# A two-layer decoder step: the weight sums of a Strassen product, three by accumulating DMAs and one on GpSimd

## The chip, the core and the metric

The kernel runs on one core of a Trainium2 chip. The metric is the device time of one execution in microseconds, median of three runs. A core has TensorE (PE, with its weight loads shown as PEld), VectorE (DVE), ScalarE (ACT), GpSimd (POOL) and SyncE (SP). SP issues nearly all loads. GpSimd computes elementwise and also issues the accumulating DMAs, which read a tile in on-chip memory and add it to another. Each engine works through its own instructions in order.

## What is computed

One step of a decoder with two layers for 576 tokens (512 of a prompt, 64 sampled). Of each layer only two products matter here: the gates of the merge, and the first product of the feed-forward block.

```
proj = (h @ lw['w_in']).astype(f32)          # 1024 of its columns for each of four gate blocks
gates = jax.nn.sigmoid(gate_logits.reshape(B, L, N_BRANCH, D_MODEL))
merged = jnp.sum(gates * up, axis=2).astype(h.dtype)
y = merged @ lw['w_out']
...
h = _rmsnorm(x, lw['ffn_norm'])
g, u = jnp.split(h @ lw['w_ffn_in'], 2, axis=-1)
x = x + ((jax.nn.silu(g) * u) @ lw['w_ffn_out']).astype(x.dtype)
```

The model width is 1024, so a product sums over 8 blocks of 128 rows; the feed-forward width is 2816, that is 22 blocks of 128 columns for `g` and 22 for `u`.

## The kernel before

Every float32 operand is split into two float16 parts, high and low. ScalarE writes the high part (L1692), VectorE the low part (L1693, it reads both the float32 source and the high part), and TensorE makes three matmuls for each block (L1718 to L1720: high by high, high by low, low by high).

**Strassen pairs.** Two column blocks of 128 are taken as one pair, cut in two along the rows: `a11`, `a12` are the two halves of the rows of the first column block, `a21`, `a22` those of the second. Each is a tile of 128 x 512 float32 (256 KB). The tokens are cut into two halves of 288. Instead of eight products of halves the pair takes seven: three with the weights themselves (A11, A12, A22) and four with sums of weights (S1 to S4). Each product is 12 matmuls of 128 x 128 by 288 columns, so a pair has 84. There are 27 pairs in a layer: 8 in the stage of the last two gate blocks (`last_gates`) and 19 in the feed-forward stage (`ffn`, column blocks 3 to 21).

**The preparation of a pair** is the generator `strassen_weights` (L1684). It loads the four tiles, then makes the sums in place, each in a step of its own:

- step 2, L1698: `a21 += a22`, by an accumulating DMA that GpSimd issues (S1)
- step 3: A11 is split, then GpSimd computes `a11 = a21 - a11` (S2)
- step 4: A22 is split, then GpSimd computes `a22 = a22 - a11` (S3)
- step 5: A12 is split, then GpSimd computes `a12 = a12 - a11` (S4)
- steps 6 to 9: S2, S1, S3 and S4 are split (`hS` tiles)

The three sums on GpSimd go through the helper at L1696. A sum overwrites the tile that a split has just read, so it waits for VectorE's low part.

**The products of a pair** are made by `strassen` (L1708) in the order A11, A12, A22, S2, S1, S3, S4. After each product one step of the preparations is taken: the first four steps split S2, S1, S3, S4 of the pair at hand, the last four run steps 2 to 5 of the next pair. VectorE combines the products (`plus`, L1734): `u2 = p1 + S2`, `u4 = u2 + S1`, and so on. In the gate stage ScalarE then takes the tanh of each result (L1529), and VectorE multiplies it with the branch's product (`gu`, L1539). In the feed-forward stage follow the silu (`fsg`, L1763) and the product (`fy`, L1765).

**Order and buffers.** A scheduler places the instructions of each engine; the order is fixed before the run. The loads of a pair are issued two pairs ahead, on SP. The tiles come from rings: "raw" has 4 buffers, "w" 4, "rd" 2 of 512 KB. In the feed-forward stage even column blocks take three raw and one w tile (L1787), odd ones two rd tiles (L1779). A load into a buffer waits until the buffer's last reader or writer is done. Matmuls write to PSUM rings; ring "b" has 4 buffers and "g" and "r" 2 each, and a buffer comes free when VectorE or ScalarE has read it.

Of the kernel before, what the change touches and what calls it, by code (L numbers as in the profile page):

```python
# [16 lines left out]
ADD, SUB, MUL, MAX, MIN = ALU.add, ALU.subtract, ALU.mult, ALU.max, ALU.min  # L17
# [157 lines left out]
class Net:  # L175
# [14 lines left out]
    def t(self, ring, shape, name, dt=F32):  # L190

        assert int(np.prod(shape[1:])) * (2 if dt == F16 else 4) <= SIZE[ring], (shape, name)
        return self.rings[ring].tile(list(shape), dt, tag=ring, name=name)
# [51 lines left out]
    def split(self, out_hi, out_lo, src, scale=1.0):  # L245

        nc = self.nc
        nc.scalar.activation(out_hi, src, AF.Copy, scale=scale)
        if scale == 1.0:
            nc.vector.tensor_tensor(out_lo, src, out_hi, op=SUB)  # L250
        else:
            nc.vector.scalar_tensor_tensor(out_lo, src, scale, out_hi, op0=MUL, op1=SUB)
# [1431 lines left out]
    def strassen_weights(self, key, load, ring, **rings):  # L1684

        nc = self.nc
        a11, a12, a21, a22 = load()
        w = self.sw[key] = {}

        def split(name, a):  # L1690
            hl = w[name] = self.t(rings.get(name, ring), [128, 2, 4, 128], "h" + name, F16)
            nc.scalar.activation(hl[:, 0], a, AF.Copy, scale=WS)  # L1692
            nc.vector.scalar_tensor_tensor(hl[:, 1], a, WS, hl[:, 0], op0=MUL, op1=SUB)  # L1693

        def add(dst, a, b, op):
            nc.gpsimd.tensor_tensor(dst, a, b, op=op)  # L1696
        yield
        nc.gpsimd.dma_start(out=a21, in_=a22, accum_op=ADD)  # L1698
        yield
        for name, a, op0, op1 in (("A11", a11, a21, a11), ("A22", a22, a22, a11), ("A12", a12, a12, a11)):  # L1700
            split(name, a)
            add(a, op0, op1, SUB)
            yield
        for name, a in (("S2", a11), ("S1", a21), ("S3", a22), ("S4", a12)):
            split(name, a)
            yield

    def strassen(self, w, t, prep, ps3, ring, then=None):  # L1708


        nc = self.nc
        h0, h1 = slice(0, HW), slice(HW, T)

        def product(ring, a, rhs):
            ps = self.psum(ring, [128, HW], "fs" + a)
            for k in range(4):
                hi, lo = rhs(k)
                nc.tensor.matmul(ps, w[a][:, 0, k], hi, start=k == 0, stop=False)  # L1718
                nc.tensor.matmul(ps, w[a][:, 0, k], lo, start=False, stop=False)  # L1719
                nc.tensor.matmul(ps, w[a][:, 1, k], hi, start=False, stop=k == 3)  # L1720
                if k % 2:
                    yield
            next(prep, None)
            return ps

        def b(o, hs):
            return lambda k: (self.h[k + o][:, 0, hs], self.h[k + o][:, 1, hs])

        def tt(i):
            return lambda k: t(i, k)  # L1730

        def plus(a, p, name):
            o = self.t(ring if name[1] == "c" else "gt", [128, HW], name)
            nc.vector.tensor_tensor(o, a, p, op=ADD)  # L1734
            if then and name[1] == "c":
                then(o)
            return o
        p1 = self.t("gt", [128, HW], "sp1")
        nc.scalar.copy(p1, (yield from product("b", "A11", b(0, h0))))
        c11 = plus(p1, (yield from product("b", "A12", b(4, h0))), "sc11")  # L1740
        p4 = yield from product("g", "A22", tt(3))
        u2 = plus(p1, (yield from product("b", "S2", tt(1))), "su2")
        p5 = yield from product("g", "S1", tt(0))
        u4 = plus(u2, p5, "su4")
        u3 = plus(u2, (yield from product(ps3, "S3", tt(2))), "su3")
        c22 = plus(u3, p5, "sc22")
        c21 = plus(u3, p4, "sc21")
        c12 = plus(u4, (yield from product(ps3, "S4", b(4, h1))), "sc12")
        return c11, c12, c21, c22
# [193 lines left out]
```

## Time and profile before

| what | value |
|---|---|
| time before, median of 3 runs | 2242.47 us (2237.26 to 2242.92) |
| profiled execution, its own time | 2235.82 us |
| its span, first to last instruction | 2234.1 us |
| busy share of the span | TensorE 92%, VectorE 75%, ScalarE 48%, GpSimd 29% |
| mean granted TensorE clock | 0.975 of full speed |
| gate stage of the pairs, layer 0 and 1 | about 536 to 677 us and 1629 to 1773 us |
| feed-forward stage of the pairs, layer 0 and 1 | about 782 to 988 us and 1878 to 2086 us |

The profile is of one execution; the rows read from it stand in a section below. Busy time of TensorE is modelled: a matmul is shown as 0.29 us long, while in a full stretch a new one starts every 0.12 us. Idle time is shown in brackets behind a row, with the engine whose work ended it.

### The profile page before, as it was taken

What the parts mean: (1) busy time and instruction counts of PE and PEld (TensorE: products, weight loads), DVE (VectorE), ACT (ScalarE), POOL (GpSimd) and SP (SyncE); (2) the same over time, 40 slices, a digit from 0 to 9 for tenths busy, and PEclk for the clock granted to TensorE, in tenths of its full rate; (3) what the DMA queues carried; (4) which work ended last, traced back from release to release, by engine and by line L of the source; (5) the groups of instructions that cost most, each with busy time, mean ns of one, the idle gap of its engine ahead of it and who ended that gap; (6) DMA issues with size and microseconds to landing.
All of it is one profiled execution on the core that took longest, in us unless ns stands there. A gap on an engine that the chain in (4) does not pass through costs nothing.

```text
span 2234.1 us, 42266 instructions
## 1 busy us (share of the span) xinstructions
PE 2047.3 (92%) x15754; PEld 1616.7 (72%) x15754; DVE 1677.4 (75%) x3719; ACT 1070.6 (48%) x2400; POOL 652.0 (29%) x850
## 2 busy tenths in 40 slices
PE   7988899898989999999998889889998988999998
PEld 5766676686767677777776667768776766777776
DVE  7889856868786899973488996686687768998531
ACT  6554545436454655442466344363554455554332
POOL 2212212245550544320011131222365415443000
PEclk9999999999999999999999999999999999999999
DMA  6312213333436244343421222142344443443431
GB/s 179 82 36 66 54 52 91 94 77 84 108 100 200 59 118 126 88 132 108 120 69 51 54 56 60 51 116 72 79 98 104 124 144 93 118 116 93 126 105 50
DMA packets 373497, 209.58 MB, mean 94 GB/s; under 512 B 59810, under 2 KB 360410, under 8 KB 373292
## 3 DMA queue, kind: packets, MB, share of 16 engines
q1 hardware_dynamic: 365516, 192.73, 31.1%
q0 software_dynamic: 7776, 14.16, 3.5%
q8 instruction: 124, 2.03, 0.4%
q14 instruction: 81, 0.66, 0.1%
HBM read 173.72 MB, written 16.59 MB: 85 GB/s over the span
## 4 chain that ended last, share of the span: by engine, by line
PE 47%; DVE 31%; ACT 8%; issue 7%; DMA 4%; POOL 3%; SPq 0%; DVEq 0%; ACTq 0%; POOLq 0%
PE pb L243 4%; PE pb L241 4%; PE pb L242 4%; PE xb L243 4%; PE xb L242 4%; PE xb L241 4%; DVE hA L1693 3%; DVE hS L1693 2%; DVE whl L229 2%; DVE sc L1734 2%; DVE fy L1765 2%; DVE qg L1111 2%; PE fsS L1720 2%; PE fsS L1718 2%; PE fsS L1719 2%
## 5 line engine op out<-in xcount | busy, mean ns | idle before, releaser
L241 PE MATMUL pb<-h,whl 128*128 128x288 f16 (+1 forms) x1504 | 439.9, 293 | 3.7 <-ACT h L463 2.2
L243 PE MATMUL pb<-h,whl 128*128 128x288 f16 (+1 forms) x1504 | 439.7, 293 | 2.7 <-DVE whl L229 2.7
L242 PE MATMUL pb<-h,whl 128*128 128x288 f16 (+1 forms) x1504 | 439.5, 292 | 0.6 <-DVE h L464 0.4
L229 DVE SCALAR_TENSOR_TENSOR whl<-raw,whl 128x512 f16<-128x512 f32 (+1 forms) x352 | 251.7, 725 | 132.0 <-ACT whl L228 130.3
L243 PEld LDWEIGHTS <-whl 128*128 128x128 f16 (+1 forms) x2784 | 277.3, 100 | 88.4 <-issue 11.0
L242 PEld LDWEIGHTS <-whl 128*128 128x128 f16 (+1 forms) x2784 | 276.7, 99 | 87.4 <-issue 11.0
L241 PEld LDWEIGHTS <-whl 128*128 128x128 f16 (+1 forms) x2784 | 279.0, 100 | 77.0 <-issue 3.6
L228 ACT ACTIVATE whl<-raw 128x512 f16<-128x512 f32 (+1 forms) x352 | 213.0, 616 | 167.4 <-PE pb L243 58.1
L243 PE MATMUL xb<-fa,whl 128*128 128x288 f16 x704 | 201.3, 286 | 0.0
L242 PE MATMUL xb<-fa,whl 128*128 128x288 f16 x704 | 201.3, 286 | 0.0
L241 PE MATMUL xb<-fa,whl 128*128 128x288 f16 x704 | 201.3, 286 | 0.0
L1718 PE MATMUL fsA<-h,hA 128*128 128x288 f16 x432 | 123.5, 286 | 14.4 <-DVE gu L1539 9.1
L1718 PE MATMUL fsS<-st,hS 128*128 128x288 f16 x456 | 131.1, 287 | 6.0 <-ACT hS L1692 6.0
L1720 PE MATMUL fsS<-st,hS 128*128 128x288 f16 x456 | 131.2, 288 | 0.9 <-DVE hS L1693 0.9
L1719 PE MATMUL fsS<-st,hS 128*128 128x288 f16 x456 | 131.1, 287 | 0.0
L1720 PE MATMUL fsA<-h,hA 128*128 128x288 f16 x432 | 123.6, 286 | 1.6 <-DVE hA L1693 1.6
L1719 PE MATMUL fsA<-h,hA 128*128 128x288 f16 x432 | 123.5, 286 | 0.0
L1696 POOL TENSOR_TENSOR raw<-raw 128x512 f32<-128x512 f32 x52 | 79.5, 1529 | 133.8 <-DVE hA L1693 129.7
L1718 PEld LDWEIGHTS <-hS 128*128 128x128 f16 x864 | 85.1, 99 | 35.5 <-ACT hS L1692 14.1
L1693 DVE SCALAR_TENSOR_TENSOR hA<-sraw,hA 128x512 f16<-128x512 f32 x110 | 101.5, 930 | 10.4 <-ACT hA L1692 9.7
L1696 POOL TENSOR_TENSOR sraw<-sraw 128x512 f32<-128x512 f32 x60 | 89.9, 1501 | 50.0 <-DVE hA L1693 45.5
L1720 PEld LDWEIGHTS <-hS 128*128 128x128 f16 x864 | 85.2, 99 | 24.6 <-DVE hS L1693 3.0
(487 smaller groups left out, 5271.1 us busy)
## 6 DMA issues: line engine op xcount, KB each, us to landing
raw<-in_w_in SPq DMA_DIRECT2D x208, 256.0 KB
sraw<-in_w_ffn_in SPq DMA_DIRECT2D x40, 512.0 KB
raw<-in_w_ffn_out SPq DMA_DIRECT2D x80, 256.0 KB
raw<-in_w_ffn_in SPq DMA_DIRECT2D x78, 256.0 KB
x<-xd SPq DMA_DIRECT2D x32, 288.0 KB
raw<-sraw POOLq DMA_DIRECT2D x34, 256.0 KB, 3.3
sraw<-in_w_in SPq DMA_DIRECT2D x32, 256.0 KB
raw<-in_w_out SPq DMA_DIRECT2D x32, 256.0 KB
```

Source lines behind the costliest of these rows:

```text
L228: nc.scalar.activation(hl[:, 0, :n], raw[:, :n], AF.Copy, scale=WS)
L229: nc.vector.scalar_tensor_tensor(hl[:, 1, :n], raw[:, :n], WS, hl[:, 0, :n], op0=MUL, op1=SUB)
L241: nc.tensor.matmul(ps, wh, hi, start=i == 0, stop=False)
L242: nc.tensor.matmul(ps, wh, lo, start=False, stop=False)
L243: nc.tensor.matmul(ps, wl, hi, start=False, stop=i == len(ks) - 1)
L1111: nc.vector.tensor_tensor(qo, qq, ee, op=MUL)
L1693: nc.vector.scalar_tensor_tensor(hl[:, 1], a, WS, hl[:, 0], op0=MUL, op1=SUB)
L1696: nc.gpsimd.tensor_tensor(dst, a, b, op=op)
L1718: nc.tensor.matmul(ps, w[a][:, 0, k], hi, start=k == 0, stop=False)
L1719: nc.tensor.matmul(ps, w[a][:, 0, k], lo, start=False, stop=False)
L1720: nc.tensor.matmul(ps, w[a][:, 1, k], hi, start=False, stop=k == 3)
L1734: nc.vector.tensor_tensor(o, a, p, op=ADD)
```

## The change

Before, one sum of a pair was an accumulating DMA and three were subtractions on GpSimd. After, S1 stays as it was; S2 stays on GpSimd, with its sign turned round (`a11 = a11 - a21`); S3 and S4 become accumulating DMAs of the turned `a11` (`a22 += a11`, `a12 += a11`). The sign of S2 is taken back where its product is used: `u2 = p1 - S2`. The values are the same sums. So in each of 54 pairs two GpSimd subtractions of 128 x 512 become two DMAs of 256 KB that GpSimd issues. All accumulating DMAs now stand at one line (L1696 of the changed kernel), the one subtraction at L1701, and lines further down are numbered 5 higher.

```diff
@@ strassen_weights
-        def add(dst, a, b, op):
-            nc.gpsimd.tensor_tensor(dst, a, b, op=op)
-        yield
-        nc.gpsimd.dma_start(out=a21, in_=a22, accum_op=ADD)
-        yield
-        for name, a, op0, op1 in (("A11", a11, a21, a11), ("A22", a22, a22, a11), ("A12", a12, a12, a11)):
-            split(name, a)
-            add(a, op0, op1, SUB)
-            yield
+        def add(dst, a):
+            nc.gpsimd.dma_start(out=dst, in_=a, accum_op=ADD)
+        yield
+        add(a21, a22)
+        yield
+        split("A11", a11)
+        nc.gpsimd.tensor_tensor(a11, a11, a21, op=SUB)
+        yield
+        split("A22", a22)
+        add(a22, a11)
+        yield
+        split("A12", a12)
+        add(a12, a11)
+        yield
@@ strassen
-        def plus(a, p, name):
+        def plus(a, p, name, op=ADD):
             o = self.t(ring if name[1] == "c" else "gt", [128, HW], name)
-            nc.vector.tensor_tensor(o, a, p, op=ADD)
+            nc.vector.tensor_tensor(o, a, p, op=op)
...
-        u2 = plus(p1, (yield from product("b", "S2", tt(1))), "su2")
+        u2 = plus(p1, (yield from product("b", "S2", tt(1))), "su2", SUB)
```

The scheduler's order changes too. In the feed-forward stage it stays as it was on GpSimd, VectorE and TensorE, with DMAs in place of subtractions. On GpSimd in the middle of the first layer's feed-forward stage, before (an even pair whose tiles are numbered 1019x, and the first sum of the odd pair behind it, 1034x):

```order
L1696 TENSOR_TENSOR raw_10192<-raw_10196,raw_10192 128x512 [waits DMAHW1_49,DMASW5_49,DVE_49]
L1696 TENSOR_TENSOR sraw_10198<-sraw_10198,raw_10192 128x512 [waits DVE_49,Pool_49]
L1698 DMA sraw_10347<-sraw_10347 128x512 [waits DMAHW1_49]
L1696 TENSOR_TENSOR raw_10194<-raw_10194,raw_10192 128x512 [waits DMAHW4_49,DVE_49]
L1698 DMA raw_10498<-sraw_10500 128x512 [waits DMAHW3_49,DVE_49]
```

and after:

```order
L1701 TENSOR_TENSOR raw_10192<-raw_10192,raw_10196 128x512 [waits DMAHW1_49,DMASW5_49,DVE_49]
L1696 DMA sraw_10198<-raw_10192 128x512 [waits DVE_49,Pool_49]
L1696 DMA sraw_10347<-sraw_10347 128x512 [waits DMAHW1_49,DMASW7_49,DMASW6_49]
L1696 DMA raw_10194<-raw_10192 128x512 [waits DMASW4_49,DMAHW4_49,DMASW2_49,DVE_49]
L1696 DMA raw_10498<-sraw_10500 128x512 [waits DMAHW3_49,DVE_49]
```

Nothing moved; the rows are S2, S3, S1 of the next pair, S4, and S1 of the pair after that. Three DMAs now stand behind one another.

In the gate stage the order differs at several places. One is on TensorE, where the last pair of block "rt" meets the first of block "rw" (`fsS3_7749` and `fsS4_7774` belong to the pair at hand, `fsS3_7943` to the next one; layer 1 has the same place). Before:

```order
L1720 MATMUL fsS3_7749<-mt5_6514,hS3_7708 128x288
L1718 LDWEIGHTS hS3_7902 [waits Activation_49]
L1718 MATMUL fsS3_7943<-mt4_6513,hS3_7902 128x288
L1719 LDWEIGHTS hS3_7902
L1719 MATMUL fsS3_7943<-mt4_6513,hS3_7902 128x288
L1720 LDWEIGHTS hS3_7902 [waits DVE_49]
L1720 MATMUL fsS3_7943<-mt4_6513,hS3_7902 128x288
L1718 LDWEIGHTS hS3_7902
L1718 MATMUL fsS3_7943<-mt4_6513,hS3_7902 128x288
L1719 LDWEIGHTS hS3_7902
L1719 MATMUL fsS3_7943<-mt4_6513,hS3_7902 128x288
L1718 LDWEIGHTS hS4_7724
```

and after:

```order
L1725 MATMUL fsS3_7749<-mt5_6514,hS3_7708 128x288
L1723 LDWEIGHTS hS4_7724 [waits Activation_49]
L1723 MATMUL fsS4_7774<-h4_143,hS4_7724 128x288 [waits Activation_49]
L1724 LDWEIGHTS hS4_7724
L1724 MATMUL fsS4_7774<-h4_143,hS4_7724 128x288
L1725 LDWEIGHTS hS4_7724 [waits DVE_49]
```

Five matmuls of the next pair's S3 stood ahead of S4 of the pair at hand; after, they stand with the other seven of their product, behind the next pair's S1.

At the same place on ScalarE, before:

```order
L1692 ACTIVATE hS3_7902<-sraw_7656 128x512 [waits PE_49,Pool_49]
L1505 ACTIVATE bhl_7607<-braw_7605 128x256 [waits DMAHW5_49]
L1739 COPY sp1_7658<-fsA11_7659 128x288
L1529 ACTIVATE sc11_7692<-sc11_7692 128x288 [waits DVE_49]
L1692 ACTIVATE hS4_7918<-sraw_7652 128x512 [waits PE_49,Activation_49]
L1529 ACTIVATE sc22_7768<-sc22_7768 128x288 [waits DVE_49]
```

and after:

```order
L1505 ACTIVATE bhl_7607<-braw_7605 128x256 [waits DMAHW5_49]
L1744 COPY sp1_7658<-fsA11_7659 128x288
L1529 ACTIVATE sc11_7692<-sc11_7692 128x288 [waits DVE_49]
L1692 ACTIVATE hS3_7902<-sraw_7656 128x512 [waits DMASW7_49,PE_49]
L1692 ACTIVATE hS4_7918<-sraw_7652 128x512 [waits DMASW6_49,PE_49,Activation_49]
L1529 ACTIVATE sc22_7768<-sc22_7768 128x288 [waits DVE_49]
```

The split of S3 moved behind the tanh of `sc11`, and both splits now wait for a DMA's landing (DMASW) where one waited for GpSimd; the tanh of `sc22` stays behind them.

## Rows read from the trace of the kernel before

**Rows 1.** Page: the chain that ended last, share of the span by engine.
```profile
PE 47%; DVE 31%; ACT 8%; issue 7%; DMA 4%; POOL 3%; SPq 0%; DVEq 0%; ACTq 0%; POOLq 0%
```

**Rows 2.** A stretch of the feed-forward stage: PE, PEld, DVE, ACT, POOL; clock, DMA, GB/s.
```profile
830.00:880.00 50.00, 47.20 (x382) 37.16 (x380) 49.86 (x82) 26.82 (x56) 23.52 (x18) 1.00 0.42 108
```

**Rows 3.** Waits of TensorE, feed-forward stage of layer 0: total, times, longest, us.
```profile
PE fsA L1718 <- DVE sc L1734: 5.4, 8, 1.0
```

**Rows 4.** Timeline of ScalarE: start, duration; the same copy in pairs four apart.
```profile
849.93 0.38 ACT L1739 COPY sp<-fsA 128x288 f32<-128x288 f32 x1
...
894.41 0.38 ACT L1739 COPY sp<-fsA 128x288 f32<-128x288 f32 x1
```

**Rows 5.** Timeline of TensorE: first matmuls of A22, of the S2 behind it, of the next S4.
```profile
859.34 0.28 PE L1718 MATMUL fsA<-st,hA 128*128 128x288 f16 x1 [0.99 <-DVE sc L1734]
...
860.81 0.29 PE L1718 MATMUL fsS<-st,hS 128*128 128x288 f16 x1
...
876.09 0.29 PE L1718 MATMUL fsS<-h,hS 128*128 128x288 f16 x1
```

**Rows 6.** Groups of VectorE instructions from 783 to 983 us: busy us, mean ns.
```profile
L1765 DVE SCALAR_TENSOR_TENSOR fy<-sc,fsg 128x288 f32<-128x288 f32 x36 | 33.1, 918 | 0.5
L1693 DVE SCALAR_TENSOR_TENSOR hS<-sraw,hS 128x512 f16<-128x512 f32 x42 | 32.9, 784 | 0.2
L1693 DVE SCALAR_TENSOR_TENSOR hA<-sraw,hA 128x512 f16<-128x512 f32 x34 | 28.9, 857 | 0.4 <-DMA raw<-in_w_ffn_in 0.4
L1693 DVE SCALAR_TENSOR_TENSOR hS<-raw,hS 128x512 f16<-128x512 f32 x24 | 20.7, 862 | 0.1
L1693 DVE SCALAR_TENSOR_TENSOR hA<-raw,hA 128x512 f16<-128x512 f32 x16 | 17.3, 1082 | 0.0
```

**Rows 7.** Timeline of VectorE: the splits around one pair's S3 and S4.
```profile
864.67 1.39 DVE L1693 SCALAR_TENSOR_TENSOR hA<-raw,hA 128x512 f16<-128x512 f32 x1
865.98 0.68 DVE L1693 SCALAR_TENSOR_TENSOR hS<-raw,hS 128x512 f16<-128x512 f32 x1
...
866.95 1.39 DVE L1693 SCALAR_TENSOR_TENSOR hS<-raw,hS 128x512 f16<-128x512 f32 x1
...
870.44 0.69 DVE L1693 SCALAR_TENSOR_TENSOR hS<-raw,hS 128x512 f16<-128x512 f32 x1
```

**Rows 8.** Timeline of GpSimd at the same place: S3, next S1, S4, S1 behind it.
```profile
864.16 1.35 POOL L1696 TENSOR_TENSOR sraw<-sraw,raw 128x512 f32<-128x512 f32 x1 [1.06 <-DVE hA L1693]
865.51 0.88 POOL L1698 DMA_DIRECT2D sraw<-sraw  x1
866.15 1.64 POOL L1696 TENSOR_TENSOR raw<-raw 128x512 f32<-128x512 f32 x1
872.21 0.88 POOL L1698 DMA_DIRECT2D raw<-sraw  x1 [4.42 <-DVE fy L1765]
```

**Rows 9.** All accumulating DMAs, issue to landing; page: the software queue, share of 16 engines.
```profile
DMA to landing us min/median/max: 3.2/3.3/5.4
...
q0 software_dynamic: 7776, 14.16, 3.5%
```

**Rows 10.** Timelines where "rt" meets "rw", layer 0 and (last row) layer 1.
```profile
611.76 2.93 POOL L1696 TENSOR_TENSOR sraw<-sraw,raw 128x512 f32<-128x512 f32 x2
...
614.73 0.63 ACT L1692 ACTIVATE hS<-sraw 128x512 f16<-128x512 f32 x1 [1.86 <-POOL sraw L1696]
...
615.41 0.30 PE L1718 MATMUL fsS<-mt,hS 128*128 128x288 f16 x1 [3.31 <-ACT hS L1692]
...
1710.69 0.42 PE L1718 MATMUL fsS<-mt,hS 128*128 128x288 f16 x1 [3.31 <-ACT hS L1692]
```

**Rows 11.** Waits of TensorE from 600 to 677 us, gate stage of layer 0.
```profile
PE fsA L1718 <- DVE gu L1539: 4.6, 3, 2.4
PE fsS L1718 <- ACT hS L1692: 3.3, 1, 3.3
...
PE fsS L1720 <- DVE hS L1693: 0.3, 1, 0.3
```

## The prediction

> **What bounds the kernel now.** I began with the chain that ended last: TensorE holds 47% of it, VectorE 31%, GpSimd 3% [rows 1]. GpSimd's sums are thus hardly ever the last link. If they cost time, it is through what they do to TensorE and VectorE. So I read the two stages that hold the pairs.
>
> In the feed-forward stage the windows show VectorE busy for 49.86 of 50 us, with the clock at its full level [rows 2]. A pair takes (894.41 - 849.93) / 4 = 11.12 us there [rows 4]. TensorE alone would take less: 12 matmuls, from A22's first to S2's first, last 860.81 - 859.34 = 1.47 us [rows 5], so 84 last 10.29 us. The missing 0.83 us per pair is TensorE's wait for a VectorE result (`sc`), 5.4 us in 8 times [rows 3]. Counted from start to start it is 8 x 0.83 = 6.6 us a layer, since the end of a matmul is modelled. This stretch is bound by VectorE.
>
> Why is VectorE so slow there? Its splits should take 0.68 us, as at 865.98; at 864.67 and 866.95 they took 1.39 [rows 7]. Beside them GpSimd ran S3 from 864.16 and S4 from 866.15, but beside the short split only the issue of a DMA, at 865.51 [rows 8]. A subtraction on GpSimd stretches VectorE, a DMA issue does not. This is the link on which the change acts.
>
> In the gate stage TensorE waits 3.3 us once for ScalarE's split of S3, then 0.3 us for VectorE's low part, and 4.6 us in three times for VectorE's `gu` [rows 11]. The first is the five matmuls that stand ahead of S4: GpSimd's S3 and S4 of the next pair run from 611.76 to 614.69, ScalarE's split follows at 614.73, TensorE at 615.41; layer 1 waits the same 3.31 us [rows 10].
>
> **The change, part by part.**
>
> Removed: two subtractions per pair. Averaged over 36 `fy`, that is 18 pairs, the splits ran over 0.68 us by 42 x 0.10 + 34 x 0.18 + 24 x 0.18 + 16 x 0.40 = 21 us [rows 6], 1.2 us per pair; the two splits read singly lost 0.71 each, 1.4 together [rows 7]. I take 1.3. S2 stays with the same size, and the 918 ns that `fy` takes on average [rows 6] stay with it. VectorE's work per pair falls from 11.1 to 9.8 us, under TensorE's 10.29.
>
> Added: two accumulating DMAs per pair. An issue takes GpSimd 0.88 us against 1.35 and 1.64 for a sum [rows 8], but the result is there only on landing, 3.3 us after the issue in the median, 5.4 at most [rows 9]. Who waits for it? Not TensorE at once: this pair's S4 was split by 871.1 [rows 7], and its product began at 876.09 [rows 5]. It is VectorE, whose queue is in order: the low part of S4 stands in a fixed place, and `sc` and `fy` wait behind it. From the end of A12's low part (866.06) to the start of S4's (870.44) VectorE has 4.38 us, of which 0.71 was stretch [rows 7], so 3.67 of other work remain. The new way takes 3.3 for the landing and 0.63 for ScalarE's high part [rows 10], 3.93: a wait of 0.26 us. In even pairs GpSimd issues S3, the next S1 and S4 in one row; from 864.16 that puts S4's issue at 865.92, while A12's low part, unstretched, ends at 865.35. That adds 0.57, so 0.83. If the three also queue for the DMA engines, more: the queue's 3.5% of 2234 us over 54 DMAs is 1.45 us of all 16 engines each [rows 9], and issues 0.88 apart would push the third back by 2 x 0.57 = 1.14, to 1.97. So the wait lies between 0.26 and 1.97; I take 0.9, nearer to the rows without queueing, since median and shortest landing (3.3 and 3.2) lie together. VectorE then needs 9.8 + 0.9 = 10.7 us a pair, 0.4 less than now: 8 x 0.4 = 3.3 us a layer. Bounds: with 0.26 TensorE sets the pace and all 6.6 go; with 1.97 VectorE needs 11.8 and the stage loses about 5.
>
> By the Trainium skill, "DMA: Bandwidth & Descriptors", section "Anatomy of one DMA", such a DMA takes some 2.0 us and its bytes at 436 GB/s, which for 256 KB is an estimate of 2.6 us. The trace says 3.3, and that stands in the sum. By the page's figure the wait would all but vanish, and the whole sum below would be about 6 us larger.
>
> Also moved: the loads. A load into a buffer whose last reader was S4's sum now waits for S4's landing instead, at most 869.2 or so where the sum ended at 867.79. The S1 after next stood on GpSimd until 872.21 (the row names `fy`; by the order it waits for two loads as well) [rows 8]. It comes 1 to 1.5 us later, and S2 of the odd pair behind it. GpSimd idles 1.06 us between S2 and S3 for VectorE [rows 8], so about that much of a late S2 is covered. I cost it at nothing; without the cover S3 and S4 come up to 1.5 us later as well, which the bound of 1.97 for the wait stands for.
>
> The gate stage: five matmuls leave their place ahead of S4, so TensorE no longer stands there for 3.3 + 0.3 us. In exchange the tanh of `sc22` stands on ScalarE behind two landings: issues at about 611.8 and 612.6 land at 615.1 and 615.9, the split ends near 616.6. The branch products use PSUM ring "b", whose four buffers let TensorE run on into the next pair before that tanh is needed. I take 3.0 of 3.6 us a layer; bounds 3.6, and nothing if the buffers run out. The `gu` waits (4.6 us) shrink with unstretched splits and grow with landings ahead of the tanh on ScalarE: two splits per pair lose 0.7 each, a landing ends about 1.5 us after the sum did. I take 0.7 us a layer; bounds 4.6 gained and 3 lost.
>
> Sum: 2 x (3.3 + 3.0 + 0.7) = 14 us. The profiled execution took 2235.82 us, so a profile of the same luck would show about 2222. It lies 6.6 us under the median of the runs, 2242.47; against that the forecast is 2228.
>
> **The rivals.**
>
> *The DMAs queue and the kernel gets slower.* The DMA engines are 42% busy in this stretch [rows 2]. Two more DMAs of 1.45 us per 11.12 us add 26 points, to 68%. If S4 lands 4.9 us after its issue, between the median and the longest of [rows 9], the wait is 0.9 + 1.6 = 2.5 us, a pair takes 12.3, and 2 x 8 pairs lose 19 us; less the 7 of the gate stage that is +12, 2254. It decides from a wait of 1.3 us, that is from a landing of about 3.7 on average: there VectorE has lost as much as it won. For it: the 5.4 us. Against it: the median.
>
> The Trainium skill ("DMA: Bandwidth & Descriptors", "Issuing engines are not separate DMA queues") says that DMAs of all issuing engines run on the same 16 and interleave; this mechanism would follow from it. The 5.4 us agrees with that, the median hardly shows it.
>
> *Nothing moves.* The S4 wait and the later loads eat what VectorE wins, and TensorE's freed 3.6 us come back as longer waits for `gu`, since VectorE has to keep up. 2242, within 7 us. For it: VectorE is busy 49.86 of 50 us, so small waits count. Against it: 1.3 us per pair is more than the likely wait.
>
> *Everything goes.* Landings hide, TensorE sets the pace in both stages: 2 x (6.6 + 3.6 + 4.6) = 30 us, 2213. For it: VectorE's 9.8 against 10.29. Against it: the splits behind landings on ScalarE, in order.
>
> **How the numbers follow.** The forecast with partial hiding (7 to 20 us gained) has 0.50, everything 0.13, nothing 0.24, slower 0.13. A difference under 0.3%, 6.7 us, can't be told from none. Faster is thus 0.50 + 0.13 = 0.63, the same 0.24, slower 0.13. The likeliest is 2228. For 8 in 10 the range takes in the forecast, the nearer half of everything's, and most of nothing's: 2213 to 2246. The forecast's own range is 2222 to 2236.
>
> **What the profile after would show.** Right: splits in the feed-forward stage near 0.7 us where S3 and S4 stood, only `fy` still stretched; fewer waits of TensorE for `sc`, a pair near 10.7 us; the 3.3 us wait ahead of S4 gone in both layers; idle time of ScalarE before `hS` put down to DMAs. Wrong: landings of more than 4 us in the row of three; a new VectorE wait before S4's low part above 1.3 us; `gu` waits grown by what the 3.3 us gave; a longer idle time of GpSimd ahead of S1, which would mean that the loads set the pace.

## The result and the profile after

The changed kernel is slower: 2297.3 us in the median against 2241.55, ratio 1.0243 with a 95% interval of 1.0215 to 1.0271. The range ended at 2246, so the prediction missed, and on the wrong side.

The page after, the chain that ended last:

```profile
PE 43%; DVE 25%; DMA 13%; ACT 8%; issue 6%; POOL 4%; SPq 1%; DVEq 0%; POOLq 0%; ACTq 0%
```

DMAs hold 13% of the chain where they held 4% [rows 1]. The feed-forward stage of layer 0 as a whole, before and after (columns as in [rows 2]), then TensorE's waits in it after, and all accumulating DMAs with the waits for their landings:

```profile
781.50:987.90 206.40, 197.56 (x1598) 155.88 (x1598) 195.89 (x334) 102.78 (x219) 87.00 (x67) 1.00 0.42 108
```

```profile
790.40:1013.40 223.00, 203.71 (x1600) 158.78 (x1599) 179.71 (x336) 106.32 (x222) 67.75 (x67) 0.97 0.63 144
```

```profile
PE fsA L1723 <- DVE sc L1739: 13.6, 8, 4.5
```

```profile
  ACT hS L1692: 145.8, 72
...
DMA to landing us min/median/max: 3.2/3.7/6.3
```

VectorE is no longer full: it is busy for 179.71 of 223.0 us, where it was for 195.89 of 206.4. It was relieved, as predicted. Yet TensorE waits for it longer, 13.6 us against 5.4 [rows 3]. The last fence says who stands between: ScalarE's splits of sums waited 145.8 us for landings. In the list of all waits VectorE's splits waited 108.1 us in 88 times for ScalarE, where they had waited 6.2 us in 10.

TensorE also runs slower. Its busy time for the same matmuls grew from 197.56 to 203.71 us, and the granted clock of the stage fell from 1.00 to 0.97. One such fall comes right behind a wait: TensorE waited 4.53 us for `sc` until 855.35, and from 855.7 to 859.1 the granted clock is 0.50, that is 1.2 GHz in place of 2.4. Over the four pair stages TensorE's busy time grew by 19 us (650.1 to 669.2), of the 54 us by which they became longer. So about a third of the loss is TensorE at its lower clock.

How one landing reaches TensorE is seen in the timeline of a feed-forward pair, over four engines:

```profile
871.80 1.59 POOL L1701 TENSOR_TENSOR sraw<-sraw 128x512 f32<-128x512 f32 x1
873.69 1.78 POOL L1696 DMA_DIRECT2D sraw<-sraw  x2 [0.30 <-POOL sraw L1701]
...
874.09 0.69 DVE L1693 SCALAR_TENSOR_TENSOR hS<-sraw,hS 128x512 f16<-128x512 f32 x1
...
877.02 0.63 ACT L1692 ACTIVATE hS<-sraw 128x512 f16<-128x512 f32 x1 [2.45 <-DMA sraw<-sraw]
...
877.68 0.69 DVE L1693 SCALAR_TENSOR_TENSOR hS<-sraw,hS 128x512 f16<-128x512 f32 x1 [1.57 <-ACT hS L1692]
...
878.77 0.45 DVE L1739 TENSOR_TENSOR sc<-su,fsS 128x288 f32<-128x288 f32 x1
...
879.28 0.28 PE L1723 MATMUL fsA<-st,hA 128*128 128x288 f16 x1 [1.52 <-DVE sc L1739]
```

S2 ends at 873.39. S3's issue follows at 873.69 and lands 3.25 us later, and ScalarE, idle for 2.45 us, starts its split at 877.02. VectorE took S2's low part at 874.09 and then stands 1.57 us before S3's at 877.68. Behind it in its queue is `sc`, which belongs to the pair that TensorE is multiplying at that moment; TensorE's next A22 waits for it until 879.28. So a landing for the next pair holds up the pair at hand.

The gate stage, in the same way, at the second pair of block "rw":

```profile
632.18 1.54 POOL L1696 DMA_DIRECT2D sraw<-raw  x1
...
637.19 0.63 ACT L1692 ACTIVATE hS<-sraw 128x512 f16<-128x512 f32 x1 [5.19 <-DMA sraw<-raw]
637.73 0.76 ACT L1529 ACTIVATE sc<-sc 128x288 f32<-128x288 f32 x2
...
637.85 0.69 DVE L1693 SCALAR_TENSOR_TENSOR hS<-sraw,hS 128x512 f16<-128x512 f32 x1 [3.15 <-ACT hS L1692]
...
639.33 0.28 PE L1723 MATMUL fsA<-h,hA 128*128 128x288 f16 x1 [2.12 <-DVE gu L1539]
```

The third DMA of a row of three, issued at 632.18, is split at 637.19, 5 us later. The tanh stands behind that split on ScalarE, `gu` behind the low part on VectorE, TensorE behind `gu`. TensorE's waits for `gu` from 600 to 687 us are 8.2 us, against 4.6 before [rows 11].

And the place where "rt" meets "rw":

```profile
610.94 0.63 ACT L1692 ACTIVATE hS<-sraw 128x512 f16<-128x512 f32 x1 [4.35 <-DMA sraw<-raw]
...
616.45 0.28 PE L1723 MATMUL fsS<-h,hS 128*128 128x288 f16 x1 [3.21 <-ACT sp L1744]
```

The five matmuls are gone from ahead of S4, and so is their wait of 3.31 us [rows 10]. In its place TensorE waits 3.21 us for ScalarE's copy `sp`. ScalarE was 4.35 us late already, behind S4's landing at 610.94, and did the rest of its queue first.

### The profile page after: what moved, and what is told of

Read it like the earlier page. It is cut to its first block, busy times and chain, and to the rows that moved or that the text cites. A ratio compares the mean times of both kernels' runs of the same rounds, so it can differ in the third digit from the quotient of the medians.

```text
span 2287.0 us, 42474 instructions
## 1 busy us (share of the span) xinstructions
PE 2068.7 (90%) x15754; PEld 1625.3 (71%) x15754; DVE 1617.1 (71%) x3719; ACT 1075.3 (47%) x2400; POOL 585.9 (26%) x850
## 4 chain that ended last, share of the span: by engine, by line
PE 43%; DVE 25%; DMA 13%; ACT 8%; issue 6%; POOL 4%; SPq 1%; DVEq 0%; POOLq 0%; ACTq 0%
PE pb L243 4%; PE pb L241 4%; PE pb L242 4%; PE xb L243 4%; PE xb L242 4%; PE xb L241 4%; DMA sraw<-sraw 3%; DMA raw<-in_w_ffn_in 3%; DMA raw<-raw 2%; DVE whl L229 2%; DVE qg L1111 2%; DMA sraw<-raw 2%; DVE hA L1693 2%; DMA braw<-in_w_branch 1%; PE fsS L1725 1%
## 5 line engine op out<-in xcount | busy, mean ns | idle before, releaser
L1723 PE MATMUL fsA<-h,hA 128*128 128x288 f16 x432 | 126.6, 293 | 27.3 <-DVE gu L1539 19.8
L1692 ACT ACTIVATE hS<-sraw 128x512 f16<-128x512 f32 x130 | 80.2, 626 | 145.2 <-DMA sraw<-raw 70.0
L1693 DVE SCALAR_TENSOR_TENSOR hS<-sraw,hS 128x512 f16<-128x512 f32 x130 | 89.8, 692 | 82.2 <-ACT hS L1692 80.3
L1723 PE MATMUL fsS<-st,hS 128*128 128x288 f16 x456 | 133.4, 293 | 6.5 <-ACT hS L1692 6.5
L1724 PE MATMUL fsS<-st,hS 128*128 128x288 f16 x456 | 133.2, 292 | 0.0
L1725 PE MATMUL fsS<-st,hS 128*128 128x288 f16 x456 | 132.8, 291 | 0.4 <-DVE hS L1693 0.3
L1725 PE MATMUL fsA<-h,hA 128*128 128x288 f16 x432 | 126.8, 294 | 1.7 <-DVE hA L1693 1.6
L1724 PE MATMUL fsA<-h,hA 128*128 128x288 f16 x432 | 126.8, 293 | 0.0
L1724 PEld LDWEIGHTS <-hA 128*128 128x128 f16 x648 | 65.2, 101 | 77.2 <-issue 60.1
L1724 PEld LDWEIGHTS <-hS 128*128 128x128 f16 x864 | 86.0, 99 | 30.0 <-issue 6.8
```

## The experiments

All ratios are against the kernel before, run on the same chip. Stage times are from the first to the last matmul of the pairs' products in the profile: gate and feed-forward (ff) stage of layer 0, then of layer 1. They are of one execution each.

| run | median us | ratio, 95% interval | gate | ff | gate | ff |
|---|---|---|---|---|---|---|
| before | 2241.55 | | 140.9 | 206.0 | 143.4 | 207.4 |
| changed | 2297.30 | 1.0243 (1.0215 to 1.0271) | 151.1 | 222.6 | 151.8 | 226.0 |
| s3_dma | 2266.07 | 1.0126 (1.0102 to 1.0150) | 151.5 | 215.0 | 153.4 | 213.9 |
| s4_dma | 2255.53 | 1.0082 (1.0053 to 1.0112) | 144.9 | 215.9 | 145.2 | 219.3 |
| gate_only | 2256.08 | 1.0083 (1.0054 to 1.0111) | 150.3 | 206.5 | 155.2 | 208.1 |
| ffn_only | 2272.97 | 1.0162 (1.0129 to 1.0195) | 144.3 | 223.4 | 146.8 | 228.7 |
| no_sums | 2187.15 | 0.9779 (0.9760 to 0.9798) | 129.8 | 197.0 | 129.6 | 197.3 |
| idle2 | 2314.33 | 1.0347 (1.0326 to 1.0368) | 143.4 | 206.3 | 143.9 | 205.8 |
| idle2b | 2300.26 | 1.0263 (1.0242 to 1.0283) | 159.8 | 221.4 | 153.9 | 223.1 |
| raw6 | 2282.95 | 1.0207 (1.0184 to 1.0231) | 148.9 | 223.7 | 151.8 | 224.2 |
| late2 | 2257.98 | 1.0093 (1.0069 to 1.0117) | 147.3 | 216.5 | 150.5 | 215.2 |
| late2_raw6 | 2240.38 | 0.9995 (0.9983 to 1.0007) | 145.2 | 208.9 | 152.8 | 207.9 |
| before_late_raw6 | 2313.42 | 1.0329 (1.0296 to 1.0362) | 161.5 | 235.5 | 160.8 | 235.5 |
| dve2 | 2222.10 | 0.9913 (0.9895 to 0.9930) | 135.6 | 205.4 | 139.1 | 205.5 |
| dve2_idle | 2234.27 | 0.9977 (0.9963 to 0.9991) | 140.6 | 208.7 | 142.9 | 209.0 |
| dve3 | 2190.67 | 0.9780 (0.9764 to 0.9797) | 132.6 | 197.0 | 131.6 | 196.6 |
| dve4 | 2206.50 | 0.9856 (0.9830 to 0.9883) | 134.5 | 202.3 | 135.1 | 204.7 |

**Which stage (gate_only, ffn_only).** A flag keeps S3 and S4 on GpSimd in one of the stages:

```diff
+        def add2(dst, a):
+            if dma:
+                add(dst, a)
+            else:
+                nc.gpsimd.tensor_tensor(dst, dst, a, op=ADD)
```

> S3 and S4 are DMAs only in the two gate stages; in the feed-forward stages they are additions on GpSimd. If each stage pays for its own sums, the gate stages keep the 10 and 8 us that they lose in the changed kernel and the feed-forward stages lose nothing: about 2242 + 18 = 2260. If the stages lose through one another (buffers, late loads at the border), the sum of this run's loss and that of the feed-forward stages alone differs clearly from 55 us.

> S3 and S4 are DMAs only in the two feed-forward stages. If each stage pays for its own sums: 17 + 18 us lost, about 2277. Both theories (waits, traffic) expect this; it says where the loss is.

Each came within 5 us. The losses of 0.83% and 1.62% add up to the whole 2.43%: each stage pays for its own sums. The stage times of one execution are less exact than that: ffn_only's gate stages, with their sums on GpSimd, are 3.4 us longer than before as well, while TensorE's busy time in them grew by 4.3 and 2.4 us.

**Which sum (s3_dma, s4_dma).** One of the two goes back to GpSimd, in s3_dma this one:

```diff
-        add(a12, a11)
+        nc.gpsimd.tensor_tensor(a12, a12, a11, op=ADD)
```

> S3 alone is an accumulating DMA; S2 and S4 are subtractions and additions on GpSimd. Theory of waits: what costs is the landing of S4, the last sum, for which ScalarE, VectorE and the next loads wait in order. S4 is back at about 1.6 us after its start, so the feed-forward stage returns to about 206 us (223 in the changed kernel) and the whole to 2235 to 2255. Rival, traffic: what costs is the load on the 16 DMA engines and half of the added DMAs is left, so about half of the loss: near 2270, feed-forward stage near 214 us.

> S4 alone is an accumulating DMA; S3 is an addition on GpSimd. Theory of waits: the landing of S4 still stands ahead of the next loads and of ScalarE's and VectorE's next instructions, so most of the loss stays: 2270 to 2290, feed-forward stage 215 to 222 us. Rival, traffic: as much traffic as with S3 alone, so the same time as that kernel, near 2270.

Both missed the time that I gave them. I had S4 as the costly one; S3 alone costs 1.26%, S4 alone 0.82%, though the two intervals just touch. The rival's 2270 for both fits s3_dma and not s4_dma.

The difference lies in the gate stage. There S3 alone makes the whole loss (10.6 and 10.0 us; the changed kernel loses 10.2 and 8.4), while S4's 4.0 and 1.8 us are about what ffn_only shows without any added DMA there. ScalarE's waits for landings in the gate stage of layer 0, in s3_dma and then in s4_dma:

```profile
ACT hS L1692 <- DMA sraw<-raw: 16.6, 5, 4.7
```

```profile
ACT hS L1692 <- DMA sraw<-raw: 4.8, 1, 4.8
```

S3's landing is waited for five times, S4's once; the split of S4 stands later in ScalarE's queue. In the feed-forward stage S4 alone costs no less than S3 alone (9.9 and 11.9 us against 9.0 and 6.5).

Traffic is the same in both kernels, and their loss in the gate stage is not. Nor did the landings get slower in either. All accumulating DMAs of s3_dma, then of s4_dma:

```profile
DMA to landing us min/median/max: 3.2/3.3/5.4
```

```profile
DMA to landing us min/median/max: 3.2/3.3/6.0
```

The median is that of the kernel before [rows 9], and yet the two lose 30 and 19 us, 49 of the 55.

**What the relief is worth (no_sums).** S3 and S4 are left out, and their splits take A22 and A12 unsummed:

```diff
-        add(a22, a11)
...
-        add(a12, a11)
```

> S3 and S4 are left out altogether (their splits take A22 and A12 unsummed); S1 and S2 as in the changed kernel. It shows what freeing VectorE of two subtractions is worth if the sums cost nothing. By the prediction's gain side both stages become bound by TensorE: about 20 to 30 us faster than before, 2207 to 2217. Rival: VectorE's relief is worth nothing, since something else sets the pace: within 7 us of before.

It is 50 us faster than before, more than expected. In the feed-forward stage TensorE sets the pace (197 us), and the gate stage gains 11 to 14 us a layer. So the changed kernel gave away some 105 us: these 50 and the 55 of its loss.

**Traffic without a waiter (idle2, idle2b, dve2_idle).** The first two keep the sums on GpSimd and add DMAs into a spare tile; idle2b ties each to the sum ahead of it:

```diff
             add(a, op0, op1, SUB)
+            if name != "A11":
+                d = self.dum[name == "A12"]
+                nc.gpsimd.dma_start(out=d, in_=d, accum_op=ADD)
```

> The kernel before, with its three sums on GpSimd, and after S3 and after S4 one more accumulating DMA of 256 KB each, into a spare tile that nobody reads: the traffic and the issues on GpSimd of the changed kernel, without a waiter. Theory of traffic: loads and S1 land later, 25 us or more slower than before. Theory of waits (ScalarE, VectorE and loads stand behind landings): 0 to 10 us slower, for GpSimd's two issues of 0.9 us per pair.

> As the run with idle DMAs, but each of them adds a finished S3 or S4 to the spare tile, so that it stands right behind that sum on GpSimd; nobody reads the spare tile. The three sums stay on GpSimd. Traffic alone: if it makes the loss, the pair stages grow by 10 us and more each, as in the changed kernel (gate 151, feed-forward 223 us). If waits in order make it, they stay within 3 us of the kernel before (gate 141 to 144, feed-forward 206 to 209).

Neither settles it. In idle2 the scheduler, with nothing to hold them, put the DMAs at the program's start: the gate stage begins 75 us later and the stages are as before. In idle2b (`in_=a`) the stages lose as much as in the changed kernel, but by another way: loads wait for the idle DMAs' reads, and VectorE is stretched more (busy 209.5 us in the feed-forward stage of layer 0, against 195.9). Its timeline:

```profile
889.34 2.49 DVE L1696 SCALAR_TENSOR_TENSOR hS<-raw,hS 128x512 f16<-128x512 f32 x1
...
889.36 1.92 POOL L1699 TENSOR_TENSOR raw<-raw 128x512 f32<-128x512 f32 x1
```

A split that meets a sum at its start takes 2.49 us, not 1.39 [rows 7]: it ends 0.55 us after the sum does. How much a sum costs VectorE depends on where the split meets it.

So dve2_idle puts S3 and S4 on VectorE, and lets GpSimd issue the two DMAs at the same places, from split weights that nothing else holds back:

```diff
-        add(a22, a11)
+        nc.vector.tensor_tensor(a22, a22, a11, op=ADD)
+        nc.gpsimd.dma_start(out=self.dum[0], in_=w["A22"], accum_op=ADD)
```

> S3 and S4 on VectorE, and GpSimd issues two more accumulating DMAs of 256 KB per pair at the places where the changed kernel issues S3 and S4; they add split weights to a spare tile that nobody reads. Same traffic and the same instructions on GpSimd as the changed kernel, but no one waits for the landings. If traffic makes the loss, this is 25 us or more slower than S3 and S4 on VectorE without it (2222): 2247 or more. If the waits make it, it stays within 8 us: 2214 to 2230.

It lies 4 us above the band of the waits and 13 below that of traffic. The idle DMAs are float16 and have the same 256 KB. S1, now the only sum by DMA with a reader, lands hardly later than before (3.3 in the median [rows 9]). The second row is the feed-forward stage of layer 0:

```profile
DMA to landing us min/median/max: 3.2/3.4/6.6
```

```profile
779.70:988.90 209.20, 198.72 (x1600) 155.74 (x1598) 189.59 (x371) 104.01 (x220) 66.82 (x67) 1.00 0.68 150
```

The DMA engines are as busy there as in the changed kernel (0.68 against 0.63). Against dve2 the traffic and issues cost 12 us. Against the changed kernel, with as many DMAs and, in the feed-forward stage, GpSimd's instructions in the same order, it is some 60 us faster, although VectorE does two additions more per pair. Traffic is thus the small part, the waiting for landings the large one.

**Later splits and more buffers (late2, raw6, late2_raw6, before_late_raw6).** The splits of S3 and S4 take their scale from a number that VectorE writes after `sc11`; the pool of raw tiles grows:

```diff
+            late = name in ("S3", "S4")
+            nc.scalar.activation(hl[:, 0], a, AF.Copy, scale=self.scl if late else WS)
...
+            if name == "sc11":
+                nc.vector.tensor_scalar(self.scl, o[:, 0:1], 0.0, WS, op0=MUL, op1=ADD)
...
-        self.wp = pool("wraw", 4)
+        self.wp = pool("wraw", 6)
```

> The changed kernel with 6 raw buffers in place of 4 (and one buffer fewer in the ring rq of another stage): an even pair's loads no longer wait for the landing of the sums of the even pair ahead. Theory of loads: the landing of S4 holds back loads, S1 at the head of GpSimd's queue and S2 behind it, and this sets the pair's period; the feed-forward stage falls from 223 us to 212 or less. Rival, waits in order: ScalarE and VectorE stand behind the landings themselves; it stays above 218.

> The changed kernel, but the splits of S3 and S4 take their scale from a number that VectorE writes after the pair's first result (sc11), so that they stand later in the order of ScalarE and VectorE, when the sums have landed. One small VectorE instruction more per pair. Theory of waits in order: ScalarE's idle time before these splits goes, both stages come back to about the time before or under it, 2225 to 2250. Rival, loads: tiles are held longer, loads come later still; no better than the changed kernel, 2285 or more.

> The changed kernel with the later splits and with 6 raw buffers. With later splits the waits for S3 and S4 are gone from ScalarE, and what is late is S2 behind S1 of the next pair, which waits for loads. If loads are now the bound, the extra buffers help here as they did not alone: feed-forward stage from 216 us to 205 or less, whole 2235 or less. If not, it stays near 216.

> Control: the kernel before, sums on GpSimd, with the later splits of S3 and S4 and 6 raw buffers. If these two only hide landings, they do nothing for sums on GpSimd: within 0.5% of before, or slower by the added order. If they are good in themselves, it is faster than before by as much as they gave the changed kernel, and then they don't show that landings were the loss.

More buffers alone leave the feed-forward stage where it was (223.7 and 224.2), so loads do not bound the changed kernel. Later splits take 6 to 11 us from each feed-forward stage (the whole is 8 us above what I expected), and no split waits for a landing any more. ScalarE's waits in late2, of the whole program:

```profile
ACT hS L1694 <- POOL raw L1703: 38.6, 29, 2.0
```

What it waits for now is S2 on GpSimd (this row, and 37.8 us more for the other ring). With later splits the buffers do help: 7 to 8 us a feed-forward stage, and the whole is back at the time before, 3 to 5 us short of what I expected. The two waits stand one behind the other. The control rules out that the remedies are good in themselves: on the kernel before they cost 74 us, and VectorE's busy time in a feed-forward stage rises there from 196 to 210 us. Of these two kernels they help only the one that waits for landings.

**Sums on VectorE (dve2, dve3, dve4).** S3 and S4, then S2 too, then S1 too:

```diff
-        nc.gpsimd.tensor_tensor(a11, a11, a21, op=SUB)
+        nc.vector.tensor_tensor(a11, a11, a21, op=SUB)
...
-        add(a22, a11)
+        nc.vector.tensor_tensor(a22, a22, a11, op=ADD)
```

> S3 and S4 as additions on VectorE, S1 and S2 as in the changed kernel. By the stretch of about 0.7 us that each sum on GpSimd costs VectorE, an addition of about 0.6 us on VectorE itself costs it no more, and its result is there at once: within 0.5% of before or a little faster, 2215 to 2245. If it is slower by more than 1%, VectorE's own work, and not its stretch, bounds the stages.

> All three sums on VectorE, S1 as a DMA. S2 on GpSimd stretches an instruction of VectorE by 0.7 to 1.6 us too, so this should be faster than with S3 and S4 alone on VectorE: 2195 to 2235.

> All four sums on VectorE, no accumulating DMA at all. Against three sums on VectorE (2191), S1's landing of 3.3 us goes and VectorE gets 0.6 us more work per pair. The feed-forward stage is paced by TensorE there, so it stays at 197 us; the gate stage may win or lose a few: 2183 to 2200.

dve2 came out as expected. dve3, 4 us better than its band, is 49 us under the kernel before and 107 under the changed one: it beats both. A window of its feed-forward stage, and groups of VectorE's instructions there (771 to 960 us):

```profile
820.00:870.00 50.00, 50.00 (x411) 39.94 (x409) 49.72 (x104) 30.60 (x59) 4.31 (x5) 1.00 0.49 127
```

```profile
L1693 DVE SCALAR_TENSOR_TENSOR hA<-sraw,hA 128x512 f16<-128x512 f32 x34 | 22.5, 682 | 0.4 <-ACT hA L1692 0.4
...
L1770 DVE SCALAR_TENSOR_TENSOR fy<-sc,fsg 128x288 f32<-128x288 f32 x36 | 16.2, 450 | 0.6
```

TensorE starts 411 matmuls in 50 us, against 382 [rows 2]. VectorE is as busy as before, but with 104 instructions in place of 82: no split and no `fy` is stretched, 682 and 450 ns in the mean against up to 1082 and 918 [rows 6]. dve4 lies 6 us above its band: S1 on VectorE costs 16 us against dve3. VectorE was nearly full there already (49.72 of 50 us), and in dve3 no engine stood idle for S1's landing.

## Why the prediction was wrong

**VectorE's relief: right in kind, wrong in size.** Stretch by sums on GpSimd was the right mechanism, and a DMA issue does not stretch. But VectorE's busy time in the feed-forward stage fell from 195.89 to 179.71 us, that is by 0.85 us for each of 19 pairs, where I took 1.3. What the relief can bring if no landing is in the way I sized too small: the largest case, everything, had 30 us, and with the two sums left out the kernel gains 50. There a feed-forward stage gains 9 to 10 us where I had 6.6, and a gate stage 11 to 14 where I had 8.2.

**The wait: the step that failed.** I priced one wait, of VectorE before "the low part of S4", with 3.67 us of other work to cover the landing: 0.9 us a pair. S3's landing I did not price. Measured in the feed-forward stage of layer 0 of the changed kernel, VectorE's splits of sums waited for ScalarE:

```profile
DVE hS L1693 <- ACT hS L1692: 32.6, 31, 3.4
```

That is 1.7 us for each of 19 pairs, more than the 1.3 us from which, by my own sum, the kernel gets slower. In the 12 pairs whose splits stand among the same neighbours as in the timeline above, 15.7 us of it are before S3's low part, 6.0 before S4's and 6.1 before S2's. So S4's wait was about 0.5 us a pair, less than I took, and S3's, at nothing in my sum, was the largest with 1.3. Relief of 0.85 and waits of 1.7 make a pair 0.87 us longer, which is the stage's 16.6 us.

S3's low part stands in VectorE's queue close behind S2's (874.09 and 877.68 above), with only two `su` and S1's split between them, and S3's DMA can only be issued when S2 is done: most of its landing is bare. Behind it stand `su` and `sc` of the pair at hand, which TensorE needs for its next A22. I looked only at the sum that comes last. Alone, S3 costs no more than S4 in this stage: in s3_dma VectorE waits 6.5 us for its splits, but S4's sum on GpSimd still stretches it, and its busy time falls by only 1.7 us; in s4_dma it waits 19.1 us and is relieved of 11.4. Why S2 comes late was not isolated.

**TensorE's clock** had no term in my sum. It is some 19 of the 54 us that the pair stages lost.

**TensorE's five us of slack were beside the point.** It was true that a pair's S4 is split long before its own product begins. What was late was the work of another pair behind that split in an in-order queue.

**Traffic.** Landings rose from 3.3 to 3.7 us in the median, the very point from which I had the slower rival decide. It named the right side, but queueing is the smaller part: s3_dma and s4_dma lose 49 us with landings of 3.3, and DMAs that nobody reads cost 12 us in dve2_idle, of 55 lost and 50 not gained. Its 2254 was 43 us short.

**The loads** at nothing: right for the changed kernel by itself (raw6). They are the next wait once the splits are out of the way (late2 against late2_raw6).

**The gate stage.** The wait ahead of S4 went as the order of instructions showed and came back as a wait for `sp`, 3.21 us. That PSUM's "four buffers let TensorE run on" failed: the landings on ScalarE also hold the copies and tanhs that empty those buffers. By s3_dma and s4_dma it is S3's landing that costs here.

Left open: how the 50 us divide between S3 and S4, and how much of the clock's 19 us follows from which wait. That raw6 is 14 us faster than the changed kernel in the median is no finding: against the kernel before on the same chip it is 8 us, and the two intervals overlap.

## What to carry to other kernels

Before a sum is moved from an engine to a DMA, list what stands behind each of its readers in their queues, also of other work, and compare the landing (here 3.2 to 6.3 us) with the work ahead of each reader; price every such landing, not only the last one. An engine that is slowed by a neighbour's instruction may do that instruction itself in the time that the slowing costs: here 0.68 us of addition on VectorE took the place of up to 1.8 us of stretch, and its result was there at once. A DMA is a good place for a sum that is needed late, as S1 here.

## What the runs showed of the hardware

A split on VectorE, with two operands in on-chip memory, that meets a sum on GpSimd ends about 0.55 us after the sum, whether the two began together (in idle2b at 889.34 and 889.36, ends at 891.83 and 891.28) or the split 0.8 us later (in the kernel before at 866.95 and 866.15, ends at 868.34 and 867.79 [rows 7, 8]). I had read a fixed stretch of 0.7 us. The split at 865.98, beside which I saw only the issue of a DMA, also met S4's sum of 866.15; it began 0.17 us ahead of the sum and kept its 0.68 us, and the sum took 1.64 us. So one sum cost VectorE from nothing to 1.8 us. The Trainium skill ("SBUF — State Buffer", "Who interferes with whom") has the loser of the two blocked for the other's whole instruction. Rows 7 and 8 agree; in idle2b both are long (2.49 and 1.92 us), so the starts in the trace do not always tell which one loses.

Accumulating DMAs issued in a row landed later one by one: of three in the changed kernel, issued at 884.49, 885.52 and 886.10, the first (S3) was split at 887.83 and the third (S4) at 890.72, 3.3 and 4.6 us after their issues. The estimate of 2.6 us worked out from the Trainium skill's "DMA: Bandwidth & Descriptors" ("Anatomy of one DMA") appeared nowhere; the shortest of 162 took 3.2.
